# The running streams' stage of a hybrid encoder step: its tiles, its head loads, and the place of the filler and of the first two rows

## The chip, the cores and the metric

The kernel runs on one core of one Trainium2 chip. The metric is the device time of one execution in microseconds. The kernel before was timed three times, and its median is what a changed kernel is set against. One further execution was profiled.

The engines have short names: PE multiplies matrices (PEld is its weight load), DVE, ACT and POOL work on vectors, and SP issues nearly all DMA transfers. Each engine takes its instructions strictly in its program's order and waits at an instruction until its inputs and its buffer are there.

## The reference, cut to what matters

One step of a one-layer encoder for two groups of requests that share the weights: a prompt of 1,040 rows (16 meta rows and 1,024 frames), and 8 running streams with 16 new frames each, which have 272 cached rows of keys and values (16 meta, 256 past). Attention is stick-breaking, with 16 heads of 64:

```python
def stick_breaking(q, k, v, q_pos, k_pos):
    z = jnp.einsum('bqhd,bshd->bhqs', q, k) * (SB_HEAD_DIM ** -0.5)
    reach = k_pos[None, :] < q_pos[:, None]
    log_beta = jax.nn.log_sigmoid(z)
    log_keep = jnp.where(reach, jax.nn.log_sigmoid(-z), 0.0)
    later = lax.cumsum(log_keep, axis=3, reverse=True) - log_keep
    w = jnp.where(reach, jnp.exp(log_beta + later), 0.0)
    return jnp.einsum('bhqs,bshd->bqhd', w, v)
```

Beside it runs a Mamba-2 scan (SSD) over the same rows. Its output is gated, normed and projected by `w_br_ssd`; attention's by `w_br_att`; two sigmoid gates weigh the sum, `w_out` projects it, and a causal convolution FFN follows. For a stream, attention goes over 272 cached and 16 new keys.

## The kernel before, in words

Every float32 product is made of three: a number x is split into a rounded part h (a cast on ACT) and the rest l (a subtraction on DVE), and `mm3` multiplies h by h, h by l and l by h. `weights` loads a block of 128 columns (`wf`) and splits it into `wh` and `wl`.

The phases follow each other: norm and the first projections (`norm_in`), the SSD, the prompt's attention (`phase_att`), the streams' attention (`phase_smp`), the merge (`ssd_operands` builds the operands of `w_br_ssd`, `br_ssd` multiplies), the FFN. A scheduler lays out the instructions of each engine; tiles come from pools that are stacked, so a tile of a later phase lies over tiles of an earlier one and its first write waits for their last use. Which tiles those are is set by the order in which the pools are made.

**The prompt's attention** goes head by head. `head` (L690) loads KH and KL (the split keys), QS (the split queries) and makes VV (the split values), each from a pool of two buffers. It works on 8 blocks of 128 rows, four to a group. For a block i PE makes z (L719, L722), ACT takes the sigmoid into `beta` (L682), POOL masks its diagonal (L728) and makes `keep` = 1 - beta (L685), DVE runs the product scan (L686) and multiplies (L688). Then, for a group, PV: for each j PE transposes the betas (L135, wT), ACT and DVE split them (L97, L98), PE multiplies (L743, L744), and a short tail goes through `wf` (L749, L751).

**Filler.** `self.fill` is a list of projection blocks that attention does not need: keys, queries and values of later head pairs, and 16 blocks of the gate logits (`gate`). A gate block is 72 matmuls, three tiles of 24, and each tile's result goes through ACT (L670) into `s_gate`. `paced` (L966) takes blocks from the list after each head and ties a tile to a mark, one of the z matmuls, behind which it may start. The rest of the list goes to the streams' stage; the last `RESERVE` = 3 blocks are kept for its end.

**The streams' stage.** `first_queries` (L758) handles the first two rows of the prompt, which see at most 15 keys: it loads 16 keys and 2 queries of all heads, makes z, a small stick-breaking in `fb`, and 8 products with `fw` (L796). `sample_att` (L802) then loads the queries (`qhs`, `qls`), the new keys of all streams (`kxh`, `kxl`, 16 loads, L813), and the last 16 cached keys of each stream (`last`, 2 times 8 loads, L819), which PE transposes and ACT and DVE split into kx in pieces of 128 columns. For each stream and half it loads 256 rows of the cache (`ck` tiles from a pool of four buffers), transposes and splits the keys into Ksh and Ksl, to which POOL copies the 32 last keys from kx (L860), spreads the queries into a block-diagonal `qd`, and runs z, the stick-breaking and PV. The results are gathered in `od` and `aout`, and `aout` is stored in one transfer (L916). `norm_rows` (L924) turns the SSD's row sums `s_ss` into factors `r`, by a square root on ACT, for which ACT loads a table, and three Newton steps on DVE, and writes `s_rs`.

**The merge's operands.** For each of 16 blocks `ssd_operands` loads yt (L939, two buffers), multiplies by rB (L941), and scales into sh on ACT (L942) and sl on DVE (L943).

## Time and profile before

| what | value |
|---|---|
| median of 3 runs | 3040.69 us (3036.63 to 3044.58) |
| profiled execution | 3035.7 us, span 3033.7 us |
| mean granted clock of PE in it | 0.988 |
| last z matmul of head 15 | 1478.93 us |
| first filler of the streams' stage | 1517.00 us |
| last matmul of the streams' stage ends, reserved filler begins | 1694.57 us |
| `w_br_ssd` begins | 1732.82 us |

A row of the timeline reads: start, duration, engine, line, operation, output <- inputs, shapes, number of merged instructions, and in brackets how long the engine had been idle before it and who ended that. A line number in a row is one of the kernel before. Durations of matmuls overlap, so their spacing says more than their length: the filler's matmuls of 384 columns last 0.34 us each and start 0.178 us apart at full clock.

### The profile page before, as it was taken

To read this page: it belongs to the slowest core of one execution; us is meant where nothing else is said; L and a number is where in the kernel's file an instruction comes from. 1 tells how busy PE (TensorE), PEld (TensorE's weight loads), DVE (VectorE), ACT (ScalarE), POOL (GpSimd) and SP (SyncE) were. 2 spreads that over 40 slices of the span, in tenths; PEclk is the share of its full clock that TensorE was granted. 3 is DMA by queue.
4 is the path that set the end of the run, shared out by engine and by line. 5 is a ranking of instruction groups with operands and counts; after the bars stand their busy time and mean duration, and the time that the engine had idled before them with its cause. 6 is when DMAs were issued, how large, how long until landed. Compare 5 with 4: busy or idle time off the path is not lost. (4 is left out here: it accounts for less than half of the span.)

```text
span 3033.7 us, 45461 instructions
## 1 busy us (share of the span) xinstructions
PE 2926.8 (96%) x17381; PEld 2768.3 (91%) x17381; DVE 1733.1 (57%) x2625; ACT 1262.9 (42%) x2630; POOL 611.2 (20%) x967
## 2 busy tenths in 40 slices
PE   7999999999989999999799899999999999999998
PEld 5997988979879999999699899999999999999997
DVE  6467666666656777777634441346754454545447
ACT  6545435354334544554434320214534242424245
POOL 0013132131222333333323000002201010101014
PEclk9999999999999999999899999999999999999999
DMA  5436255353574554544444553536211111111113
GB/s 188 110 86 172 87 141 152 91 162 90 148 218 125 167 148 132 157 124 106 77 137 140 168 171 100 152 105 195 71 43 44 43 44 43 44 43 40 39 43 119
DMA packets 445496, 338.44 MB, mean 112 GB/s; under 512 B 43991, under 2 KB 421155, under 8 KB 445279
## 3 DMA queue, kind: packets, MB, share of 16 engines
q1 hardware_dynamic: 445279, 335.54, 38.8%
q8 instruction: 137, 2.24, 0.3%
q14 instruction: 80, 0.66, 0.1%
HBM read 244.31 MB, written 91.15 MB: 111 GB/s over the span
## 5 line engine op out<-in xcount | busy, mean ns | idle before, releaser
L115 PE MATMUL mm<-sh,wh 128*128 128x384 f32 (+3 forms) x2520 | 869.5, 346 | 14.7 <-ACT sh L942 5.2
L118 PE MATMUL mm<-sl,wh 128*128 128x384 f32 (+3 forms) x2520 | 869.8, 345 | 2.3 <-DVE sl L98 1.2
L119 PE MATMUL mm<-sh,wl 128*128 128x384 f32 (+3 forms) x2520 | 865.6, 344 | 0.0
L115 PEld LDWEIGHTS mm<-sh,wh 128*128 128x128 f32 (+1 forms) x2520 | 475.7, 189 | 29.5 <-ACT sh L942 6.4
L118 PEld LDWEIGHTS mm<-sl,wh 128*128 128x128 f32 (+1 forms) x2520 | 475.7, 189 | 15.5 <-issue 8.9
L119 PEld LDWEIGHTS mm<-sh,wl 128*128 128x128 f32 (+1 forms) x2520 | 475.5, 189 | 5.7 <-issue 3.9
L106 DVE TENSOR_TENSOR wl<-wf,wh 128x1024 fp32r<-128x1024 f32 (+2 forms) x205 | 252.6, 1233 | 318.0 <-ACT wh L105 317.8
L115 PE MATMUL mm<-ph,wh 128*128 128x386 f32 x1248 | 424.5, 340 | 2.7 <-ACT ph L97 2.0
L118 PE MATMUL mm<-pl,wh 128*128 128x386 f32 x1248 | 424.6, 341 | 0.0
L119 PE MATMUL mm<-ph,wl 128*128 128x386 f32 x1248 | 422.5, 339 | 0.2 <-DVE wl L106 0.2
L105 ACT CAST wh<-wf 128x1024 fp32r<-128x1024 f32 (+2 forms) x205 | 212.4, 1037 | 482.2 <-PE mm L118 454.5
L1151 DVE SCALAR_TENSOR_TENSOR acc<-fx,cwf,acc 128x256 f32<-128x256 f32 (+1 forms) x352 | 170.8, 516 | 154.0 <-ACT acc L1149 150.0
L115 PEld LDWEIGHTS mm<-ph,wh 128*128 128x128 f32 x1248 | 236.2, 189 | 3.9 <-ACT ph L97 2.3
L119 PEld LDWEIGHTS mm<-ph,wl 128*128 128x128 f32 x1248 | 236.2, 189 | 1.1 <-DVE wl L106 0.7
L118 PEld LDWEIGHTS mm<-pl,wh 128*128 128x128 f32 x1248 | 235.2, 188 | 1.8
L686 DVE TENSOR_TENSOR_SCAN keep<-keep 128x144 f32<-128x144 f32 (+7 forms) x128 | 179.7, 1406 | 57.9 <-POOL keep L685 57.2
L115 PE MATMUL mm<-ah,wh 128*128 128x384 f32 x528 | 179.8, 340 | 0.0
L119 PE MATMUL mm<-ah,wl 128*128 128x384 f32 x528 | 179.2, 339 | 0.0
L118 PE MATMUL mm<-al,wh 128*128 128x384 f32 x528 | 178.6, 338 | 0.0
L1078 POOL TENSOR_TENSOR sq<-sq,sq 128x386 f32<-128x386 f32 (+1 forms) x42 | 60.2, 1434 | 467.9 <-ACT sq L1077 456.4
L98 DVE TENSOR_TENSOR wTl<-wT,wTh 128x512 fp32r<-128x512 f32 (+3 forms) x176 | 103.0, 602 | 80.1 <-ACT wTh L97 79.1
L1176 DVE TENSOR_TENSOR h<-mm,h 128x384 f32<-128x384 f32 x144 | 79.8, 556 | 119.7 <-PE mm L119 119.5
(329 smaller groups left out, 4548.2 us busy)
## 6 DMA issues: line engine op xcount, KB each, us to landing
wf<-in_w_in SPq DMA_DIRECT2D x80, 512.0 KB
wf<-in_w_up SPq DMA_DIRECT2D x44, 512.0 KB
t<-s_ac SPq DMA_DIRECT2D x36, 512.0 KB
wf<-in_w_down SPq DMA_DIRECT2D x28, 512.0 KB
wf<-in_w_out SPq DMA_DIRECT2D x24, 512.0 KB
s_y<-x SPq DMA_DIRECT2D x16, 577.0 KB
yt<-s_y SPq DMA_DIRECT2D x16, 577.0 KB
KH<-s_kh SPq DMA_DIRECT2D x32, 260.0 KB
```

Source lines behind the costliest of these rows:

```text
L98: nc.vector.tensor_tensor(out=l, in0=x, in1=h.bitcast(F32), op=ALU.subtract)
L105: nc.scalar.copy(wh, wf)
L106: nc.vector.tensor_tensor(out=wl, in0=wf, in1=wh.bitcast(F32), op=ALU.subtract)
L115: i = nc.tensor.matmul(p, wh[:, k, :], mh[:, c:c + w], start=s, stop=False)
L118: nc.tensor.matmul(p, wh[:, k, :], ml[:, c:c + w], start=False, stop=False)
L119: nc.tensor.matmul(p, wl[:, k, :], mh[:, c:c + w], start=False, stop=e)
L686: nc.vector.tensor_tensor_scan(out=K[:, ::-1], data0=K[:, ::-1], data1=K[:, ::-1], initial=1.0, op0=ALU.mult, op1=ALU.min)
L1078: nc.gpsimd.tensor_tensor(out=acc[:, :w], in0=acc[:, :w], in1=sq, op=ALU.add)
L1151: nc.vector.scalar_tensor_tensor(out=op, in0=src(q), scalar=w(q), in1=op, op0=ALU.mult, op1=ALU.add)
L1176: self.nc.vector.tensor_tensor(out=h, in0=p, in1=h, op=ALU.add)
```

## The change

1. A scratch tile `s_ck` in DRAM gets the rows 256 to 272 of all streams' cached keys, by one copy of 512 KB whose place in the code is behind head 1. `last` is then loaded from it, 2 loads for 16.
2. kx becomes two pairs: kc for the cached keys, kn for the new ones. kn comes by 2 loads of all streams for 16 loads; kc is split 512 columns at a time; POOL copies two pieces of 16 keys for one of 32.
3. KH, KL, QS and VV get a pool for even and one for odd heads, one buffer each. The pools of both stages are made in another order: the streams' first tiles (`last`, qd, qs, kn, kc) lie over tiles of the last but one head, and `mixst`, `od` and `aout` come last.
4. `first_queries` is called ahead of head 15 and takes three of the four `ck` buffers for its tiles.
5. `RESERVE` is 2, and one gate block runs at the end of head 15: its first tile may start behind the last mark (z of row block 6), the second and third behind the first PV matmul of group 0 and of group 1 (`pv_marks`).
6. `norm_rows` is called ahead of `sample_att`.
7. The pool `rows` is made ahead of the pool `fill`.

```diff
-RESERVE = 3
+RESERVE = 2
...
+        self.s_ck = dr([TS, 1024], 's_ck')
...
-        KH, KL = (self.tile(ap, [128, TP], F32R, n) for n in ('KH', 'KL'))
-        QS = self.tile(ap, [128, TP - T0], F32R, 'QS')
-        VV = self.tile(ap, [128, 9, 128], F32R, 'VV')
+        KH, KL = (self.tile(ap, [128, TP], F32R, f'{n}{h % 2}', bufs=1) for n in ('KH', 'KL'))
+        QS = self.tile(ap, [128, TP - T0], F32R, f'QS{h % 2}', bufs=1)
+        VV = self.tile(ap, [128, 9, 128], F32R, f'VV{h % 2}', bufs=1)
...
-                nc.tensor.matmul(po[:, lo:], VV[:, j, :], wh[:, lo:], start=(j == 0), stop=False)
+                mm = nc.tensor.matmul(po[:, lo:], VV[:, j, :], wh[:, lo:], start=(j == 0), stop=False)
+                if j == 0:
+                    self.pv_marks = [mm] if g == 0 else self.pv_marks + [mm]
...
-        x = self.tile(ap, [128, 4, 288], F32R, 'Ksh').bitcast(F32).rearrange("p a b -> p (a b)")[:, :288]
+        x, v, Q = (self.tile(self.ckp, [128, 2, 512], F32, 'ck').rearrange("p a b -> p (a b)") for _ in range(3))
...
-        for j in range(8):
-            for t, src in zip(kx, (self.s_kh, self.s_kl)):
-                nc.sync.dma_start(t[:, j, :, 16:32].bitcast(F32),
-                                  src[128 * j:128 * j + 128, TP:T].rearrange("p (b t) -> p b t", t=16))
+        kc, kn = ([self.tile(ap, [128, 8, TS], F32R, n + x, bufs=1) for x in 'hl'] for n in ('kc', 'kn'))
+        for t, src in zip(kn, (self.s_kh, self.s_kl)):
+            nc.sync.dma_start(t.bitcast(F32), src[:, TP:T].rearrange("(j p) t -> p j t", p=128))
...
-            for b in range(NB):
-                nc.sync.dma_start(lk[16 * b:16 * b + 16], ck[b, 256:272, 512 * hf:512 * hf + 512])
+            nc.sync.dma_start(lk, self.s_ck[:, 512 * hf:512 * hf + 512])
...
-            for j in range(4):
-                self.split(h[:, j], l[:, j], v[:, j])
+            self.split(*(t[:, 4 * hf:4 * hf + 4] for t in kc), pk.rearrange("p (j s) -> p j s", j=4))
...
-                    nc.gpsimd.tensor_copy(K[:, :, 256:288], kx[x][:, 4 * hf:4 * hf + 4, b].bitcast(F32))
+                    for i, k in enumerate((kc, kn)):
+                        nc.gpsimd.tensor_copy(K[:, :, 256 + 16 * i:272 + 16 * i],
+                                              k[x][:, 4 * hf:4 * hf + 4, 16 * b:16 * b + 16].bitcast(F32))
...
-                'wTh', 'wTl', 'wf32', 'att', 'vf', 'KH', 'KL', 'QS', 'VV', 'keep', *(f'beta{i}' for i in range(8)))}
+                'KH0', 'KL0', 'QS0', 'VV0', 'vf', *(f'beta{i}' for i in range(8)), 'KH1', 'KL1', 'QS1', 'VV1', 'keep',
+                'wTh', 'wTl', 'wf32', 'att', 'fb', 'fw', 'fo')}
...
+                    if p == 7 and e == 1:
+                        self.first_queries()
...
-        self.ckp = self.pool(right, "cache", 4, side='right')
+                        self.ckp = self.pool(right, "cache", 4, side='right')
+                        self.nc.sync.dma_start(self.s_ck.rearrange("(b s) c -> b s c", s=16),
+                                               self.a['cache_k'][0, :, 256:272].rearrange("b s h d -> b s (h d)"))
+            self.fill.pop(0)([marks[-1]] + self.pv_marks)
...
-            mp = self.stp = self.pool(c2, "mixst", 3)
...
-                'aout', 'od', 'wTh', 'wTl', 'keep', 'beta', 'v', 'r', 'newton', 'qdh0', 'qhs', 'qls', 'kxh', 'kxl',
-                'last', 'V3h', 'V3l', 'qdl0', 'qdh1', 'qdl1', 'Ksh', 'Ksl', 'Vsh', 'Vsl',
-                'w30', 'w31', 'fb', 'fw', 'fo')}
+                'last', 'qdh0', 'qdl0', 'qdh1', 'qdl1', 'qhs', 'qls', 'knh', 'knl', 'kch', 'kcl', 'Ksh', 'Ksl', 'V3h', 'V3l',
+                'v', 'r', 'newton', 'beta', 'keep', 'Vsh', 'Vsl', 'w30', 'w31', 'wTh', 'wTl', 'od', 'aout')}
+            self.stp = self.pool(c2, "mixst", 3)
...
-            self.first_queries()
+            self.norm_rows(self.ap)
             self.sample_att(3 * len(self.fill) / 16)
-            self.norm_rows(self.ap)
...
+                k.rowp = k.pool(c1, "rows", 2)
                 k.stp = k.pool(c1, "fill", 7)
-                k.rowp = k.pool(c1, "rows", 2)
```

**PE at the end of head 15.** The numbers behind a name tell its buffers apart. Before, behind the last two z matmuls (L719, L722) stand group 0's last PV matmuls, the transposes of both groups and nothing else:

```order
L719 MATMUL z_15646<-KH_15486,QS_15488 128x344
L722 MATMUL z_15646<-KL_15487,QS_15488 128x344
L744 MATMUL o_15549<-wTl_15567,VV_15489 128x400
L135 MATMUL wT_15582<-ident_60,beta_2879_15523 128x128
L135 MATMUL wT_15582<-ident_60,beta_2882_15534 128x128 x2
L743 MATMUL o_15549<-wTh_15576,VV_15489 128x272
L135 MATMUL wT_15659<-ident_60,beta_2899_15594 128x128
L135 MATMUL wT_15659<-ident_60,beta_2903_15609 128x128
L135 MATMUL wT_15659<-ident_60,beta_2907_15624 128x128
L744 MATMUL o_15549<-wTl_15577,VV_15489 128x272
L751 MATMUL o_15549<-wf_2897_15586,VV_15489 128x144
L751 MATMUL o_15549<-wf_2897_15586,VV_15489 128x16
```

In the changed kernel the same z matmuls (now L720, L723) are followed by matmuls of a gate block (`mm`, L115 to L119), among which the PV and the transposes stand:

```order
L720 MATMUL z_15716<-KH_2879_15556,QS_2881_15558 128x344
L723 MATMUL z_15716<-KL_2880_15557,QS_2881_15558 128x344
L115 MATMUL mm_15913<-sh_124,wh_15908 128x384
L118 MATMUL mm_15913<-sl_125,wh_15908 128x384
L119 MATMUL mm_15913<-sh_124,wl_15909 128x384
L115 MATMUL mm_15913<-sh_126,wh_15908 128x384
L747 MATMUL o_15619<-wTl_15626,VV_2882_15559 128x512
L135 MATMUL wT_15642<-ident_60,beta_2886_15582 128x128
L135 MATMUL wT_15642<-ident_60,beta_2889_15593 128x128
L135 MATMUL wT_15642<-ident_60,beta_2892_15604 128x128
L118 MATMUL mm_15913<-sl_127,wh_15908 128x384
```

So filler now stands between the last z and the transposes that need the last beta.

**PE at the head of the streams' stage.** Before, from the last tail product of head 15 (L751) to the first filler:

```order
L751 MATMUL o_15658<-wf_2939_15739,VV_15489 128x144
L751 MATMUL o_15658<-wf_2939_15739,VV_15489 128x16
L779 MATMUL z_15966<-Ksh_15954,last_15962 32x16 x8
L135 MATMUL pk_16030<-ident_60,last_16021 128x128 x4
L135 MATMUL wT_15981<-ident_60,fb_15975 16x32
L796 MATMUL o_15985<-fw_15983,Vsh_15959 128x32 x8
L135 MATMUL pk_16052<-ident_60,last_16043 128x128 x4
L135 MATMUL pk_16115<-ident_60,ck_16103 128x128 x4
L879 MATMUL z_16134<-Ksh_16107,qdh_2968_16065 128x288
L115 MATMUL mm_16188<-sh_119,wh_16183 128x384
```

Now, from the same product (L754):

```order
L754 MATMUL o_15728<-wf_2949_15809,VV_2882_15559 128x144
L754 MATMUL o_15728<-wf_2949_15809,VV_2882_15559 128x16
L135 MATMUL pk_16141<-ident_60,last_16139 128x128 x4
L135 MATMUL pk_16150<-ident_60,last_16148 128x128 x4
L135 MATMUL pk_16209<-ident_60,ck_16195 128x128 x4
L135 MATMUL pk_16216<-ident_60,ck_16195 128x128 x4
L877 MATMUL z_16228<-Ksh_16199,qdh_2984_16157 128x288
L115 MATMUL mm_16282<-sh_120,wh_16277 128x384
```

The first two rows' z, transposition and eight products are gone from here, and both halves of `last` are transposed at once.

**ACT at the same place.** Before, `norm_rows`' table load and square root (L925) stand behind all of head 15:

```order
L749 COPY wf_2939_15739<-wT_15735 128x272
L872 CAST Vsh_16129<-ck_16105 128x1024
L753 COPY att_15743<-o_15658 64x512
L925 ACT_TABLE_LOAD
L925 ACTIVATE r_17935<-v_17934,eps_69 64x73
L783 ACT_TABLE_LOAD
L783 ACTIVATE fb_15975<-z_15966 32x16
L97 CAST kxh_16003<-pk_16030 128x8x16 x3
```

Now they (L923) stand between the last beta's sigmoid (L683) and group 0's tail `wf` (L752):

```order
L683 ACTIVATE beta_2921_15709<-z_15713 128x348
L683 ACTIVATE beta_2921_15709<-z_15716 128x344
L97 CAST wTh_15646<-wT_15642 128x272
L923 ACT_TABLE_LOAD
L923 ACTIVATE r_16116<-v_16115,eps_69 64x73
L671 ACT_TABLE_LOAD
L671 ACTIVATE st_15938<-mm_15913 128x384
L752 COPY wf_2907_15656<-wT_15652 128x272
L756 COPY att_15660<-o_15619 64x512
L97 CAST wTh_15734<-wT_15729 128x512
```

Behind them on ACT stand a gate tile's evacuation (`st`) and both groups' remaining copies.

**SP at the end of the streams' stage.** Before, the store of `aout` (L916) stands ahead of the first rB and yt:

```order
L104 DMA wf_18381<-in_w_br_ssd 128x8x128
L104 DMA wf_20719<-in_w_out 128x8x128
L104 DMA wf_20754<-in_w_out 128x8x128
L916 DMA s_att_86<-aout_15998 128x8x128
L936 DMA rB_18261<-s_rs_85 128x1154
L939 DMA yt_18263<-s_y_83 128x1154
L939 DMA yt_18270<-s_y_83 128x1154
L671 DMA s_gate_87<-st_18022 128x384
```

Now rB and the first two yt (L934, L937) stand ahead of the weights of `w_out` and of the store (L914):

```order
L104 DMA wf_18482<-in_w_br_ssd 128x8x128
L934 DMA rB_18281<-s_rs_86 128x1154
L937 DMA yt_18283<-s_y_84 128x1154
L937 DMA yt_18290<-s_y_84 128x1154
L104 DMA wf_20739<-in_w_out 128x8x128
L104 DMA wf_20774<-in_w_out 128x8x128
L914 DMA s_att_87<-aout_16128 128x8x128
L937 DMA yt_18297<-s_y_84 128x1154
```

The second pair of yt stays behind the store.

More of the change, by code (lines that the diff above doesn't have):

```diff
@@ L760, in first_queries @@
         nc, ap, pa = self.nc, self.ap, self.pa
-        x = self.tile(ap, [128, 4, 288], F32R, 'Ksh').bitcast(F32).rearrange("p a b -> p (a b)")[:, :288]
-        x = x.rearrange("p (i j t) -> p i j t", i=2, j=8)
+        x, v, Q = (self.tile(self.ckp, [128, 2, 512], F32, 'ck').rearrange("p a b -> p (a b)") for _ in range(3))
+        x = x[:, :288].rearrange("p (i j t) -> p i j t", i=2, j=8)
         for i, (qs, ks) in enumerate(((self.s_qh, self.s_kh), (self.s_ql, self.s_kl))):
@@ L765, in first_queries @@
             nc.sync.dma_start(x[:, i, :, 2:18], ks[:, 0:16].rearrange("(j p) t -> p j t", p=128))
-        v = self.tile(ap, [128, 2, 512], F32R, 'Vsh').bitcast(F32)[:16].rearrange("p a (j c) -> p (a j) c", c=128)
+        v = v[:16].rearrange("p (j c) -> p j c", c=128)
         nc.sync.dma_start(v, self.s_v[:, 0:16].rearrange("j t c -> t j c"))
         nc.vector.tensor_tensor(out=x[:, 0], in0=x[:, 0], in1=x[:, 1], op=ALU.add)
-        Q = self.tile(ap, [128, 512], F32, 'last', bufs=2)[:, :256].rearrange("p (j c) -> p j c", c=32)
+        Q = Q[:, :256].rearrange("p (j c) -> p j c", c=32)
         nc.gpsimd.memset(Q, 0.0)
@@ L776, in first_queries @@
             nc.gpsimd.tensor_copy(diagonal(Q.rearrange("p j c -> p (j c)"), e), x[64 * e:64 * e + 64, 0, :, 0:2])
-        ps = self.tile(pa, [128, 512], F32, 'z')
+        ps = self.tile(pa, [128, 512], F32, 'z', bufs=2)
         for j in range(8):
@@ L793, in first_queries @@
         nc.scalar.copy(w, pt[:16, :32])
-        po = self.tile(pa, [128, 512], F32, 'o')
+        po = self.tile(pa, [128, 512], F32, 'o', bufs=2)
         for j in range(8):
@@ L808, in sample_att @@
             nc.sync.dma_start(t.bitcast(F32), src[:, TP - T0:T2].rearrange("(j p) t -> p j t", p=128))
-        kx = [self.tile(ap, [128, 8, NB, 32], F32R, n, bufs=1) for n in ('kxh', 'kxl')]
-        for j in range(8):
-            for t, src in zip(kx, (self.s_kh, self.s_kl)):
-                nc.sync.dma_start(t[:, j, :, 16:32].bitcast(F32),
-                                  src[128 * j:128 * j + 128, TP:T].rearrange("p (b t) -> p b t", t=16))
+        kc, kn = ([self.tile(ap, [128, 8, TS], F32R, n + x, bufs=1) for x in 'hl'] for n in ('kc', 'kn'))
+        for t, src in zip(kn, (self.s_kh, self.s_kl)):
+            nc.sync.dma_start(t.bitcast(F32), src[:, TP:T].rearrange("(j p) t -> p j t", p=128))
         for hf in range(2):
             lk = self.tile(ap, [128, 512], F32, 'last', bufs=2)
-            ck = a['cache_k'][0].rearrange("b s h d -> b s (h d)")
-            for b in range(NB):
-                nc.sync.dma_start(lk[16 * b:16 * b + 16], ck[b, 256:272, 512 * hf:512 * hf + 512])
+            nc.sync.dma_start(lk, self.s_ck[:, 512 * hf:512 * hf + 512])
             pk = self.tile(pa, [128, 512], F32, 'pk', bufs=2)
```

2 lines of the change are left out of this document (removed).

## The prediction

> **What bounds the kernel now.** I read the profile's page first, then the busy time by windows, the timeline of TensorE (PE) where the windows show holes, and the lists of the other engines for who ended each wait. The page:
>
> ```profile
> PE 2926.8 (96%) x17381; PEld 2768.3 (91%) x17381; DVE 1733.1 (57%) x2625; ACT 1262.9 (42%) x2630; POOL 611.2 (20%) x967
> PEclk9999999999999999999899999999999999999999
> ```
>
> PE is busy 96% of the span and no other engine comes near. The change takes no PE work away, so it can only win where PE idles or runs at a lower granted clock. The only slice of the clock line below 9 lies in the middle, where the last head of the prompt hands over to the running streams' stage. There the windows read (busy time of each engine, granted clock, DMA share, GB/s):
>
> ```profile
> core 0: us, PE busy (x) PEld busy (x) DVE busy (x) ACT busy (x) POOL busy (x), PEclk, DMA share, GB/s
> 1480.00:1490.00 10.00, 5.18 (x25) 3.49 (x25) 7.73 (x8) 2.04 (x4) 3.87 (x5) 0.85 1.01 138
> 1490.00:1500.00 10.00, 7.87 (x33) 6.06 (x33) 3.22 (x6) 3.42 (x7) 0.41 (x2) 0.64 0.76 78
> 1500.00:1510.00 10.00, 1.66 (x25) 1.28 (x23) 3.70 (x12) 4.73 (x9) 3.88 (x8) 0.70 0.64 168
> 1510.00:1520.00 10.00, 8.97 (x36) 8.46 (x36) 3.17 (x8) 3.74 (x11) 3.17 (x7) 0.50 0.25 41
> ```
>
> Busy time times clock is 4.4 + 5.0 + 1.2 + 4.5 = 15.1 us of full-speed work in 40 us: 24.9 us are lost. With a few tenths on either side this hole costs about 26 us (the clock is not weighted by busy time, so 24 to 28). PE's timeline through it:
>
> ```profile
> 1477.79 0.40 PE L743 MATMUL o<-wTh,VV 128*128 128x512 f32 x1
> 1478.93 0.32 PE L722 MATMUL z<-KL,QS 128*128 128x344 f32 x1
> ...
> 1486.61 0.45 PE L135 MATMUL wT<-ident,beta 128*128 128x128 f32 x2 [3.13 <-DVE beta L688]
> 1487.62 0.80 PE L743 MATMUL o<-wTh,VV 128*128 128x512 f32 x1 [0.56 <-ACT wTh L97]
> ...
> 1493.86 0.79 PE L744 MATMUL o<-wTl,VV 128*128 128x512 f32 x1 [1.74 <-DVE wTl L98]
> ...
> 1501.90 0.63 PE L135 MATMUL pk<-ident,last 128*128 128x128 f32 x4 [0.99 <-DMA last<-in_cache_k]
> 1509.87 0.21 PE L135 MATMUL wT<-ident,fb 32*16 32x32 f32 x1 [7.34 <-DVE fb L789]
> 1510.34 3.62 PE L796 MATMUL o<-fw,Vsh 16*128 16x32 f32 x16 [0.26 <-ACT fw L793]
> ...
> 1516.62 0.58 PE L879 MATMUL z<-Ksh,qdh 128*128 128x288 f32 x1 [0.77 <-ACT Ksh L97]
> 1517.00 0.52 PE L115 MATMUL mm<-sh,wh 128*128 128x384 f32 x1
> ...
> 1521.11 0.34 PE L118 MATMUL mm<-sl,wh 128*128 128x384 f32 x1
> ...
> 1522.00 0.34 PE L115 MATMUL mm<-sh,wh 128*128 128x384 f32 x1
> ```
>
> Head 15 has no filler. After its last z matmul (1478.93) PE waits for the last row block's chain on POOL and DVE until 1486.61. Then come its seven PV steps without cover, and the first two rows' little attention, which holds PE 7.34 us for `fb`. Filler begins at 1517.00, at half clock. From 1521.11 to 1522.00 five filler matmuls start, 0.178 us each, so a gate block of 72 is 12.8 us of cover.
>
> **Term 1, the last head and the stage's head.** The change puts one gate block into the hole. Its first tile comes behind row block 6's z and spreads over the 7.4 us up to 1486.61: some 32 filler matmuls (5.7 us) and group 0's own PV work fill that. The rest stands between the last transposes and the first two PV steps. The first two rows' matmuls (2.5 us or so of work) go ahead of head 15, into filler of head 14 and 15, and the 7.34 us wait for `fb` goes with them. ACT and DVE carry less there too:
>
> ```profile
> 1499.50 1.05 ACT L872 CAST Vsh<-ck 128x1024 fp32r<-128x1024 f32 x1
> ...
> 1505.33 1.28 ACT L925 ACT_TABLE_LOAD   x1 [4.17 <-DMA v<-s_ss]
> ...
> 1515.89 0.59 ACT L97 CAST Ksh<-pk 128x512 fp32r<-128x512 f32 x1 [0.19 <-PE pk L135]
> ```
>
> ```profile
> 1495.38 4.93 SPq L819 DMA_DIRECT2D last<-in_cache_k  x8
> ...
> 1501.50 0.47 SPq L924 DMA_DIRECT2D v<-s_ss  x1
> ```
>
> Two loads from the scratch tile replace the two rows of eight (4.93 us of issue for one of them), two loads of 512-byte runs replace sixteen of 64-byte runs, and the splits of kx go from four a half to one.
>
> What stays lost afterwards, worked out: (i) five full PV steps of group 1 nearly without filler, each a hand-over PE to ACT (0.59) to DVE to PE, with a weight split (1.05 on ACT) among them: 3 us, bounds 1.5 and 6, from the single wait of 1.74 above taken once to three times. (ii) The hand-over to the first stream: behind the last PV matmul ACT copies `att`, casts two Vsh (2 x 1.05) and two kch (2 x 0.59), then Ksh (0.59), about 4.4 us in order, with only transposes for PE: 4 us, bounds 2 and 6. (iii) Filler at half clock behind it: before, the 13 starts from 1517.00 to 1521.11 took 4.1 us instead of 2.3, so 1.8 us (0 to 3.6). That is 9 us, so the term is 26 - 9 = **-17 us**, bounds -24 (28 less 4) and -11.
>
> Whether (iii) is due hangs on how long a gap must be. Before, the gap of 3.13 us was followed by a 512-column matmul of 0.80 us where the same took 0.40 at 1477.79. The Trainium skill ("TensorE: Matmul & The Clock Gate", What's actually happening) says that the clock falls to half after an idle window of about 3.4 us, the window running free. By that rule a gap that I have at 4 us may or may not hold a whole window, and the sum would be 1.8 us lower where it doesn't; the trace's gap of 3.13 us, with shorter ones around it, was enough, so I keep the cost.
>
> **Term 2, norm_rows in the last head.** Its chain cost ACT 1.28 + a second table load + the wait for `v`: issued at 1501.50, ACT free at 1505.33, 3.8 us. Now ACT sits there behind the last z, ahead of group 0's `wf`, and DVE's r steps stand ahead of all wTl of group 1. From the last z to the first PV of group 1 PE has some 39 filler matmuls (6.9 us) and about 2.6 us of group 0's work and transposes, 9.5 us; ACT's way is 3.8 + 1.28 + 0.4 + 1.28 and three copies of about 0.5, 8.3 us. Hidden with about 1 us to spare: 0, bounds 0 and +4.
>
> **Term 3, the merge head.** Two blocks instead of three are left to cover the building of w_br_ssd's operands. Before:
>
> ```profile
> 1735.00:1740.00 5.00, 2.33 (x10) 1.31 (x8) 3.06 (x3) 1.64 (x2) 0.00 (x0) 0.95 0.81 285
> 1740.00:1745.00 5.00, 2.65 (x9) 2.57 (x9) 3.64 (x3) 2.58 (x3) 0.00 (x0) 0.50 0.85 254
> 1745.00:1750.00 5.00, 5.00 (x27) 5.00 (x26) 1.36 (x1) 1.13 (x1) 0.00 (x0) 0.87 1.02 345
> ```
>
> ```profile
> 1680.13 0.29 PE L883 MATMUL z<-Ksh,qdl 128*128 128x288 f32 x1
> ...
> 1694.57 0.42 PE L115 MATMUL mm<-sh,wh 128*128 128x384 f32 x1
> ...
> 1769.76 0.44 PE L115 MATMUL mm<-sh,wh 128*128 128x384 f32 x1 [1.22 <-ACT sh L942]
> ```
>
> ```profile
> 1695.31 0.37 SPq L916 DMA_DIRECT2D s_att<-aout  x1
> ...
> 1701.52 0.81 SPq L939 DMA_DIRECT2D yt<-s_y  x2
> 1702.38 7.02 SPq L671 DMA_DIRECT2D s_gate<-st  x2
> ```
>
> ```profile
> 1709.29 1.26 ACT L942 ACTIVATE sh<-yt,gv 128x1154 fp32r<-128x1154 f32 x1 [0.24 <-DVE yt L941]
> ```
>
> ```profile
> 1709.18 2.84 DVE L943 SCALAR_TENSOR_TENSOR sl<-yt,gv,sh 128x1154 fp32r<-128x1154 f32 x2
> ```
>
> The same product gives 2.2 + 1.3 + 4.4 = 7.9 us of work in 15: 7.1 lost, plus 1.22: 8.3 us. One block less takes away 12.8 us of cover. What pays for it: `aout`, `od` and `mixst` move to the end of the stage's stack, so the first two yt loads no longer stand behind the store of `aout` (1695.31, which before they followed by 6.2 us) but wait for the last z (1680.13). Two yt buffers make a chain of pairs. Before, the first pair was done at 1709.18 + 2.84 = 1712.0, 17.4 us behind the stage's end at 1694.57. Now yt times rB can be done before the end, and what is left behind the last copies of `aout` (about 0.5) is one sh of 1.26, beside the second of which the two sl of 1.42 begin, 4.6 us in all: 12.8 us earlier. Later pairs gain more if SP is not held at the gate stores as at 1702.38 (7.02 us): up to 19 us earlier. Lost afterwards 8.3 + 12.8 - (12.8 to 19) = 8.3 to 2.1, middle 5: **-3 us**, bounds -8.3 (nothing lost) and +12.8 (no load earlier).
>
> **Term 4, the start.** The copy into `s_ck` (512 KB) waits for nothing, and its issue stands ahead of the loads of x, on which PE waits:
>
> ```profile
> 14.70 2.10 SPq L238 DMA_DIRECT2D x<-in_x_prompt  x3
> ```
>
> ```profile
> 20.39 0.55 PE L135 MATMUL tp<-ident,x 128*128 128x128 f32 x3 [1.71 <-DMA x<-in_x_prompt]
> ```
>
> ```profile
> 10.00:20.00 10.00, 8.03 (x35) 5.73 (x33) 7.58 (x30) 8.70 (x22) 0.39 (x2) 1.00 0.86 243
> ```
>
> At 243 GB/s 512 KB are 2.2 us of a transfer that is 0.86 busy already: **+2 us**, bounds 0 (other matmuls fill it) and +4 (read and write both counted). The Trainium skill ("DMA: Bandwidth & Descriptors", Rules for kernel authors) speaks against this form: an outermost dimension of fewer than 16 confines a transfer to that many engines, and this one has 8. By it the copy takes twice as long but leaves eight engines free; the sum would stay inside those bounds, and no row here shows such a copy.
>
> **Edits at nothing.** 32 more POOL copies, each half as wide as this one:
>
> ```profile
> 1520.45 0.29 POOL L860 CAST Ksh<-kxh 128x128 fp32r<-128x128 f32 x1 [3.19 <-ACT kxh L97]
> ```
>
> At most 32 x 0.29 = 9.3 us over the stage's 174 us (1521 to 1694.57), on an engine at 20% overall; without cover they would cost PE at most that. I take 0, -2 to +2. The heads' two pools by parity hold the same two buffers. The new order of att's pools shifts head 0's loads at the SSD's end, where PE loses time already:
>
> ```profile
> 840.00:850.00 10.00, 4.90 (x31) 2.57 (x32) 5.10 (x11) 8.92 (x23) 1.18 (x2) 0.83 0.49 135
> ```
>
> That 5.10 us of missing PE time can shrink or grow by most of itself: 0, -4 to +4.
>
> **The sum.** -17 + 0 - 3 + 2 + 0 = -18. The profiled run took 3035.7 us (span 3033.7 and 2.0 around it), 5.0 below the median of the three shown, 3040.7. So 3035.7 - 18 = 3017.7 on its own scale, and **3022.7 us**, say 3023, against the median. A difference of 0.3%, 9.1 us, is about what can be told from none: faster means under 3031.6, slower over 3049.8.
>
> **The rivals.**
> (a) *The cover is missed at the merge.* The yt loads come no earlier, because what they now lie over is released late, or the queue is held at a weight load ahead of them: +12.8 instead of -3, so -18 + 15.8 = -2, 3038. For it: SP issues in order and was held 7.02 us at 1702.38. Against: in the new order the first yt loads stand ahead of the w_out weights and the `aout` store. Chance 0.1.
> (b) *The hole stays.* The new tiles still wait for head 15, or the PV tail and hand-over are at the long ends of (i) and (ii), so half of 17 is won: -9.5, 3031, on the edge of no change. For it: `knl` and `qhs` are still loaded behind the last z. Against: `last` and its two splits no longer wait for anything of head 15. Chance 0.12.
> (c) *The slow side: ACT held at the load of `v` in the last head.* ACT runs in order; while it waits for `v`, it evacuates neither `wf` nor filler nor wTh, and PE starves once the 1 us to spare is used. `v` is issued behind a cache load, the store of `fo` and a weight load. Every us past 3.8 + 1 = 4.8 costs one; slower than before by 9.1 needs 18 + 9.1 = 27 of them, a wait of 32 us. At 40 us: 35 - 18 = +17, 3058. For it: all loads of this place share one queue, and a weight load ahead of `v` has to find its buffer free. Against: the wait of before was 4.17 (row at 1505.33). Chance 0.06, with anything else on that side.
> (d) *It does not do what it says*: PE's order keeps the filler out of the hole. Against: the order of PE's program has those matmuls there. Chance 0.02, 3040 or above.
>
> **How the numbers follow.** The forecast's own case has 0.70. Half the widths of its terms are 6.5, 2, 5.5, 2, 2 and 4 us; they are independent, so the root of the sum of squares, 10 us, is what they make together: 3013 to 3033. To leave out no more than 2 in 10 of all cases the range goes half as far again: 3008 to 3037, which takes in nearly all of the own case (0.67), most of (b) and the near part of (a). Faster: 0.64 of the 0.70 lies under 3031.6, half of (b) and a third of (a) with a larger term 1: 0.73. Same: the rest of these three and (d), 0.06 + 0.06 + 0.07 + 0.02 = 0.21. Slower: (c), 0.06.
>
> **What would show it.** Right: from the last z of head 15 to full-clock filler in the streams' stage PE is busy at clock 1.00 but for about 9 us, with no wait for `fb`; one gap of about 4 us ahead of the first z of stream 0; yt's first loads issued before the store of `aout`; waits in w_br_ssd of about 5 us. Wrong: a wait of ACT for `v` above 5 us with PE idle behind it; the first yt load behind the stage's end; a transposition of x waiting more than 4 us at the start; or gaps grown elsewhere inside the streams' stage.

## The result, and the profile after

The changed kernel takes 3003.75 us (median of 5 runs, 3002.16 to 3011.89), the kernel before 3040.56 us (5 runs, 3036.45 to 3044.58). The ratio is 0.9885, with a 95% interval from 0.9867 to 0.9903: about 37 us faster, twice what was forecast and 4 us below the range's lower end (two more comparisons of the same program, e12 and e3 below, give 32 and 31 us). The profiled execution took 3004.2 us; its span, 3002.4, is 31.3 shorter than that of before. The page of the changed kernel:

```profile
PE 2915.3 (97%) x17381; PEld 2763.2 (92%) x17381; DVE 1729.5 (58%) x2619; ACT 1262.0 (42%) x2624; POOL 614.6 (20%) x999
PEclk9999999999999999999999999999999999999998
```

PE does the same matmuls, and the slice below 9 in the middle is gone. Where the time went is read by following the same matmul through both profiles. Each row of the table is the start of one matmul; the offset is after minus before, and the last column is how much the offset changed since the row above.

| matmul | before | after | offset | change of this part |
|---|---|---|---|---|
| first transposition of the SSD (`sio`) | 126.1 | 128.4 | +2.3 | +2.3 |
| its last transposition of `cs` | 755.7 | 757.0 | +1.3 | -1.0 |
| first PV of attention (wTh, VV) | 929.5 | 924.0 | -5.5 | -6.8 |
| last z of head 15 | 1478.9 | 1476.6 | -2.3 | +3.2, holds the first two rows' matmuls, 2.5 or so |
| first z of the streams | 1516.6 | 1507.3 | -9.3 | -7.0, holds one block more (12.8) |
| last transposition of the stage | 1694.2 | 1681.1 | -13.1 | -3.8 |
| first norm sum of the FFN | 2089.1 | 2057.4 | -31.7 | -18.6, holds one block less |

So, with the block's 12.8 us put to one side: start +2.3, the SSD and its end -7.8, the last head and the stage's head -16.6, the stage -3.8, the merge -5.8: -31.7.

PE through the former hole, in the changed kernel (the rows that answer to those of before from the last z on):

```profile
1476.60 0.32 PE L723 MATMUL z<-KL,QS 128*128 128x344 f32 x1
...
1486.22 0.64 PE L754 MATMUL o<-wf,VV 128*128 128x144 f32 x4 [1.32 <-ACT wf L752]
...
1500.14 1.07 PE L135 MATMUL pk<-ident,last 128*128 128x128 f32 x8
1504.19 1.25 PE L135 MATMUL pk<-ident,ck 128*128 128x128 f32 x8 [2.98 <-DVE kcl L98]
1507.27 0.61 PE L877 MATMUL z<-Ksh,qdh 128*128 128x288 f32 x1 [1.82 <-POOL Ksh L857]
...
1512.47 0.37 PE L115 MATMUL mm<-sh,wh 128*128 128x384 f32 x1
1512.68 0.34 PE L118 MATMUL mm<-sl,wh 128*128 128x384 f32 x1
```

No wait for the last beta and none for `fb` is left. Three waits above 0.3 us are: one for ACT's `wf`, and two in the hand-over to the first stream, 4.8 us together, behind which filler runs at half clock (granted clock 0.50) until 1512.47. The windows (columns as before):

```profile
1475.00:1485.00 10.00, 9.91 (x62) 9.34 (x61) 7.61 (x10) 4.45 (x9) 1.35 (x2) 1.00 0.57 125
1485.00:1495.00 10.00, 8.74 (x54) 8.13 (x54) 3.40 (x9) 4.68 (x10) 0.00 (x0) 1.00 0.18 54
1495.00:1505.00 10.00, 6.71 (x41) 5.02 (x42) 6.55 (x10) 6.55 (x12) 5.88 (x17) 1.00 0.56 153
1505.00:1515.00 10.00, 8.18 (x37) 7.94 (x36) 2.67 (x4) 2.30 (x4) 3.16 (x9) 0.66 0.53 164
```

By busy time times clock 0.1 + 1.3 + 3.3 + 4.6 = 9.3 us are lost in 40 (9.2 in finer windows, where the kernel before loses 25.8 from 1475 to 1525 us by the same count; 7.7 in e12).

ACT behind the last z, with `norm_rows` in it, and the first yt loads at the stage's end on SP, whose last z starts at 1666.5:

```profile
1478.63 1.28 ACT L923 ACT_TABLE_LOAD   x1
1483.73 0.36 ACT L923 ACTIVATE r<-v,eps 64x73 f32<-64x73 f32 x1 [3.82 <-DMA v<-s_ss]
1484.11 1.28 ACT L671 ACT_TABLE_LOAD   x1
1485.40 0.49 ACT L671 ACTIVATE st<-mm 128x384 f32<-128x384 f32 x1
1485.79 0.38 ACT L752 COPY wf<-wT 128x272 f32<-128x272 f32 x1
```

```profile
1663.33 0.32 SPq L934 DMA_DIRECT2D rB<-s_rs  x1
1666.66 0.80 SPq L937 DMA_DIRECT2D yt<-s_y  x2
1667.51 4.09 SPq L104 DMA_DIRECT2D wf<-in_w_out  x2
1682.21 0.37 SPq L914 DMA_DIRECT2D s_att<-aout  x1
```

The two yt loads are issued right behind the last z and 15.6 us ahead of the store. In the merge PE then waits four times for under 0.9 us instead of 1.65, 1.02, 2.35 and 1.22. Then the start, and the window in the SSD's end, for which the prediction had taken no change:

```profile
25.01 0.90 PE L135 MATMUL tp<-ident,x 128*128 128x128 f32 x3 [4.29 <-DMA x<-in_x_prompt]
```

```profile
840.00:850.00 10.00, 7.99 (x59) 5.93 (x58) 5.46 (x11) 7.71 (x22) 3.43 (x4) 1.00 0.70 194
```

The matmul behind that hole, first before, then after:

```profile
845.41 2.05 PE L473 MATMUL st<-xe,bt 128*128 128x512 f32 x2 [5.10 <-ACT bt L456]
```

```profile
844.81 1.10 PE L474 MATMUL st<-xe,bt 128*128 128x512 f32 x2 [2.02 <-issue]
```

PE waits 4.29 us for x at the start where it waited 1.71, and the hole at 845 us is 2.0 instead of 5.1 us. Before, half clock follows it (matmuls of 2.05 us together where they now take 1.10), so the window loses 2.0 us of work now and lost 5.9.

### The profile page after: what moved, and what is told of

Its sections match the earlier page's. It is cut to its first block, busy times and chain, and to the rows that moved or that the text cites. A ratio compares the mean times of both kernels' runs of the same rounds, so it can differ in the third digit from the quotient of the medians.

```text
span 3002.4 us, 45455 instructions
## 1 busy us (share of the span) xinstructions
PE 2915.3 (97%) x17381; PEld 2763.2 (92%) x17381; DVE 1729.5 (58%) x2619; ACT 1262.0 (42%) x2624; POOL 614.6 (20%) x999
## 4 chain that ended last, share of the span: by engine, by line
PE 80%; DMA 8%; DVE 5%; ACT 3%; issue 2%; POOL 1%; SPq 0%; POOLq 0%; ACTq 0%; DVEq 0%
PE mm L115 22%; PE mm L118 22%; PE mm L119 22%; PE wT L135 3%; DMA t<-s_ac 2%; DMA yt<-s_y 1%; PE yd L489 1%; PE z L720 1%; PE o L747 1%; PE z L723 1%; DMA out_ssm_sample<-t 1%; PE o L744 1%; PE st L474 1%; DMA wf<-in_w_out 1%; PE px L135 1%
## 5 line engine op out<-in xcount | busy, mean ns | idle before, releaser
L115 PE MATMUL mm<-sh,wh 128*128 128x384 f32 (+3 forms) x2520 | 866.7, 345 | 9.2 <-ACT xp L369 3.7
L119 PE MATMUL mm<-sh,wl 128*128 128x384 f32 (+3 forms) x2520 | 865.2, 344 | 0.0
L115 PEld LDWEIGHTS mm<-sh,wh 128*128 128x128 f32 (+1 forms) x2520 | 474.6, 188 | 22.3 <-issue 5.9
L119 PEld LDWEIGHTS mm<-sh,wl 128*128 128x128 f32 (+1 forms) x2520 | 475.0, 188 | 5.6 <-issue 3.9
L115 PE MATMUL mm<-ph,wh 128*128 128x386 f32 x1248 | 424.4, 340 | 2.0 <-ACT ph L97 2.0
L119 PE MATMUL mm<-ph,wl 128*128 128x386 f32 x1248 | 422.6, 339 | 1.1 <-DVE wl L106 1.1
L1155 DVE SCALAR_TENSOR_TENSOR acc<-fx,cwf,acc 128x384 f32<-128x384 f32 (+2 forms) x352 | 170.8, 515 | 154.6 <-ACT acc L1153 150.6
L115 PEld LDWEIGHTS mm<-ph,wh 128*128 128x128 f32 x1248 | 236.2, 189 | 2.9 <-ACT ph L97 2.3
L119 PEld LDWEIGHTS mm<-ph,wl 128*128 128x128 f32 x1248 | 236.2, 189 | 1.8 <-DVE wl L106 1.4
L115 PE MATMUL mm<-ah,wh 128*128 128x384 f32 x528 | 179.8, 340 | 0.0
L119 PE MATMUL mm<-ah,wl 128*128 128x384 f32 x528 | 179.2, 339 | 0.0
```

The lines of the kernel that those rows point to most:

```text
L115: i = nc.tensor.matmul(p, wh[:, k, :], mh[:, c:c + w], start=s, stop=False)
L119: nc.tensor.matmul(p, wl[:, k, :], mh[:, c:c + w], start=False, stop=e)
L1155: nc.vector.scalar_tensor_tensor(out=op, in0=src(q), scalar=w(q), in1=op, op0=ALU.mult, op1=ALU.add)
```

## The experiments

All ratios are to the kernel before, timed anew on the same chip in each comparison; between the comparisons its median moves from 3033.1 to 3040.6 us. Offsets are those of the profiled run to the kernel before, as in the table.

**The block (e1).**

```diff
-RESERVE = 2
+RESERVE = 3
...
-            self.fill.pop(0)([marks[-1]] + self.pv_marks)
```

> The changed kernel without the gate block at the end of head 15, and with three blocks reserved again. Theory A (the block is what fills the hole): the time lost by PE between the last z of head 15 and full-clock filler, 9 us in the changed kernel, grows by 10 to 13 us, the merge head loses its 3 us less, and the time is 7 to 10 us above the changed kernel's. Rival B (the early loads, the merged splits and the moved queries made the gain, and the block only stands in for waits that are gone anyway): the head loses at most 4 us more, and the time is within 2 us of the changed kernel's.

Ratio 0.9924 (0.9909 to 0.9939), 3012.0 us. The profiled run took 3012.0, 8 us above the changed kernel's. PE waits again where it did:

```profile
1480.33 0.64 PE L754 MATMUL o<-wf,VV 128*128 128x144 f32 x4 [2.68 <-ACT wf L752]
1485.98 0.69 PE L135 MATMUL wT<-ident,beta 128*128 128x128 f32 x2 [4.41 <-DVE beta L689]
...
1501.24 1.79 PE L135 MATMUL pk<-ident,ck 128*128 128x128 f32 x8 [3.70 <-DVE kcl L98]
```

Windows from 1475 to 1525 us lose 17.1 us instead of 9.2 (7.7 in e12): theory A for the hole, with 8 to 9 us for the growth, a little less than its 10. The other half of the hole's 16.6 us was won without the block. And the merge, with its third block back, waits no less (1.75 and 1.28 us): so a third block there would win nothing.

**The first two rows (e2).**

```diff
-                    if p == 7 and e == 1:
-                        self.first_queries()
...
+            self.first_queries()
             self.norm_rows(self.ap)
```

> The changed kernel with the first two rows' attention called at the head of the streams' stage again. Theory A (its chain of waits is not covered there): 5 to 10 us above the changed kernel, with a wait for fb of several us on PE behind the last PV. Rival B (the hand-over to the first stream, about 5 us of PE waiting anyway, hides the chain): at most 2 us above it, no more than its 2.5 us of matmuls.

Ratio 0.9923 (0.9908 to 0.9938), 3012.1 us. From the first PV of attention to the stage's end it takes 3.7 us longer than the changed kernel's first profile, and 6.9 longer than that of e12. Both programs have the rows' matmuls in this stretch, so the difference lies in waits and in half clock:

```profile
1505.51 0.18 PE L135 MATMUL wT<-ident,fb 32*16 32x32 f32 x1 [1.18 <-POOL Ksl L857]
1508.72 0.58 PE L877 MATMUL z<-Ksh,qdh 128*128 128x288 f32 x1 [3.02 <-ACT Ksh L97]
```

There is no 7-us wait for `fb`: with its loads long done, the chain mostly lies beside the hand-over, as B had it. The total would speak for A, but nearly 4 us of it stand ahead of the first PV, where both programs are the same, and 3 in the merge. So the move itself is worth 4 to 7 us at its place, in one profile against two.

**norm_rows (e3).**

```diff
-            self.norm_rows(self.ap)
             self.sample_att(3 * len(self.fill) / 16)
+            self.norm_rows(self.ap)
```

> The changed kernel with norm_rows called behind the streams' attention again, as before. Theory A (its wait for v and its steps are hidden in the last head): within 2 us of the changed kernel, and PE's gap ahead of the tail product of group 0 (1.3 us) goes. Rival B (its place costs the last head, as the slow side of the prediction had it): 2 to 5 us below the changed kernel. Rival C (its table loads and wait then fall into the hand-over to the first stream): 3 to 6 us above.

Ratio 0.9904 (0.9884 to 0.9923), 3006.0 us; the profiled span is 1.8 us longer. But the edit changes nothing: the scheduler laid out the same list of instructions on every engine, and `norm_rows`' square root on ACT still stands in head 15, at 1482.9. So none of the theories is tested, and the run is one more profile of the changed kernel. PE's wait for `wf` is only 0.17 us there because `v` came earlier (ACT waits 2.68 us for it instead of 3.82); the two of the hand-over are 2.98 and 2.31. Item 6 of the change thus has no effect by itself beside the other items.

**The pools of attention, alone (e4).** The kernel before with these lines of the change:

```diff
+        KH, KL = (self.tile(ap, [128, TP], F32R, f'{n}{h % 2}', bufs=1) for n in ('KH', 'KL'))
+        QS = self.tile(ap, [128, TP - T0], F32R, f'QS{h % 2}', bufs=1)
+        VV = self.tile(ap, [128, 9, 128], F32R, f'VV{h % 2}', bufs=1)
...
+                'KH0', 'KL0', 'QS0', 'VV0', 'vf', *(f'beta{i}' for i in range(8)), 'KH1', 'KL1', 'QS1', 'VV1', 'keep',
+                'wTh', 'wTl', 'wf32', 'att')}
...
+                k.rowp = k.pool(c1, "rows", 2)
                 k.stp = k.pool(c1, "fill", 7)
```

> The kernel before with only the tiles' overlay at the start of attention changed: KH, KL, QS and VV in pools by parity of the head, the order of attention's pools, and rows ahead of fill. Theory A (these pools alone let head 0's loads start earlier at the SSD's end): PE's loss between 840 and 950 us falls from 14 to about 9 us, the time is 6 to 8 us below the kernel before, all of it by the first PV matmul. Rival B (the gain there comes from the scheduler's other order, set off by the scratch copy or the moved queries): within 2 us of the kernel before.

Ratio 1.0022 (1.0012 to 1.0031): slower. But at the first PV of attention the offset is -6.5 us, and the window of the hole reads:

```profile
840.00:850.00 10.00, 8.11 (x57) 5.77 (x56) 5.60 (x9) 8.74 (x23) 3.46 (x3) 1.00 0.64 193
```

So theory A holds at its place, and its total is wrong: with the streams' pools in their old order the gain is lost again at the end of attention. They now lie over other tiles there, which is the likely reason but was not tested alone. The last z of head 15 stands at -2.3, the first z of the streams at +4.1, behind a longer wait for the last beta (3.13 us before) and a new one for `last`:

```profile
1488.50 0.69 PE L135 MATMUL wT<-ident,beta 128*128 128x128 f32 x2 [6.91 <-DVE beta L688]
...
1506.62 1.04 PE L779 MATMUL z<-Ksh,last 128*32 128x16 f32 x16 [7.47 <-POOL last L776]
```

What shrank the hole can be seen on ACT. Its list there is held at the load of `t` (9.07 us before, 8.06 in the changed kernel); PE's matmul of `bt` comes behind it. Before:

```profile
840.41 2.44 ACT L483 ACTIVATE t<-t,tok 128x128 f32<-128x128 f32 x8 [9.07 <-DMA t<-s_ac]
842.76 1.03 ACT L105 CAST wh<-wf 128x1024 fp32r<-128x1024 f32 x1
843.69 0.48 ACT L560 ACTIVATE st<-mm 128x386 f32<-128x386 f32 x1
844.08 1.04 ACT L484 ACTIVATE t<-t 128x1024 f32<-128x1024 f32 x1
845.02 0.24 ACT L456 COPY bt<-ms 128x128 f32<-128x128 f32 x1
```

After:

```profile
832.07 1.05 ACT L105 CAST wh<-wf 128x1024 fp32r<-128x1024 f32 x1
833.01 0.50 ACT L561 ACTIVATE st<-mm 128x386 f32<-128x386 f32 x1
...
842.12 2.44 ACT L484 ACTIVATE t<-t,tok 128x128 f32<-128x128 f32 x8 [8.06 <-DMA t<-s_ac]
844.47 0.24 ACT L457 COPY bt<-ms 128x128 f32<-128x128 f32 x1
844.61 1.05 ACT L485 ACTIVATE t<-t 128x1024 f32<-128x1024 f32 x1
```

The scheduler laid the engines' lists out anew, and `bt` came to stand right behind the step that waits: of the three longer steps that stood between, two now go ahead of the wait and one behind `bt`. ACT has the same order in e4. That the lists changed because attention's first tiles became free at other times is how the scheduler works out its times, and not shown by a run of its own.

**The copy into s_ck (e5).**

```diff
+                        self.issue_after(cp, marks[-1])
```

> The changed kernel with the copy into s_ck tied behind the last z mark of head 1, so that its issue stands in the middle of attention and not at the start. Theory A (the copy's bytes, ahead of the loads of x, cost 2 to 4 us at the start): 2 to 3 us below the changed kernel, with the offset gone by 130 us. Rival B (the start lost time by a chance reordering or by the load of the memory): within 1 us of it.

Ratio 0.9893 (0.9877 to 0.991), 3004.3 us. At its place theory A holds: PE waits 1.79 us for x instead of 4.29, and the offset at 126 us is -1.1 instead of +2.3. In the total nothing of these 3.4 us is seen. They are gone by the first PV of attention (offset -4.8, the changed kernel's -5.5), where the same matmuls come at other times from profile to profile; and the merge is 4.5 us longer than in the first profile of the changed kernel, whose repetition (e12) is 2.7 longer there too. The cause at the start stands firm even so: in the eleven profiles with the copy there, e12 among them, the offset at 126 us is +0.6 to +4.0, and in the three without it (before, e4, e5) -1.1 to +0.8.

**rB and the yt loads (e6).**

```diff
+            if g == 0:
+                self.issue_after(d, self.att_store)
...
+                if b < 2:
+                    self.issue_after(d, self.att_store)
```

> The changed kernel with the first rB and the first two yt loads ordered behind the store of aout on SP again, all else as it is. Theory A (these loads' place pays for the block that is missing at the merge): the merge head is 8 to 13 us longer, and so the time. Rival B (the operands' chain is held elsewhere, by its later pairs or by ACT's order with the gate evacuations): at most 4 us longer.

Ratio 0.992 (0.9898 to 0.9941), 3011.8 us. rB and the first two yt stand behind the store, these at 1683.5:

```profile
1683.49 1.11 SPq L939 DMA_DIRECT2D yt<-s_y  x2
1686.76 8.30 SPq L672 DMA_DIRECT2D s_gate<-st  x2
```

The offset is -12.9 at the stage's end, as in the changed kernel, and -23.0 at the FFN's first norm sum where that has -31.7. The merge is 8.5 us longer: theory A. The order in which three loads are issued is worth that much.

**rows and fill (e8).**

```diff
-                k.rowp = k.pool(c1, "rows", 2)
                 k.stp = k.pool(c1, "fill", 7)
+                k.rowp = k.pool(c1, "rows", 2)
```

> The changed kernel with the pool rows behind the pool fill, as before, so that the streams' first tiles (last, qs) lie over other tiles, and last is loaded behind the last head's filler. Theory A (the early loads of last matter): the wait ahead of the first transposes at the streams' head grows, 2 to 5 us above the changed kernel. Rival B (last is there in time all the same): within 1.5 us. For the gain at the SSD's end, 5 us of PE's loss between 840 and 950: if it stays, it belongs to the pools of KH, KL, QS and VV; if it goes, to the place of rows.

Ratio 0.9906 (0.9884 to 0.9927), 3005.4 us, the profiled span 0.1 us from the changed kernel's. `last` is waited for (1.89 us), but the wait behind it is 1.47 instead of 2.98, and the other is gone: B. From 755 us to the first PV of attention it wins 5.4 us, so that gain does not need `rows` in its new place: with e4 it belongs to attention's own pools. Whether to the pairs by parity or to the order of the others was not separated.

**The third tile later (e9), and qhs early (e11, e10).** e9 lets the third tile start behind group 1's last product:

```diff
-                if j == 0:
-                    self.pv_marks = [mm] if g == 0 else self.pv_marks + [mm]
+                if j == 0 and g == 0:
+                    self.pv_marks = [mm]
...
+            if g == 1:
+                self.pv_marks = self.pv_marks + [mm]
```

e11 only reorders the streams' pools; e10 does both.

```diff
-                'last', 'qdh0', 'qdl0', 'qdh1', 'qdl1', 'qhs', 'qls', 'knh', 'knl', 'kch', 'kcl', 'Ksh', 'Ksl', 'V3h', 'V3l',
-                'v', 'r', 'newton', 'beta', 'keep', 'Vsh', 'Vsl', 'w30', 'w31', 'wTh', 'wTl', 'od', 'aout')}
+                'last', 'V3h', 'V3l', 'w30', 'w31', 'beta', 'keep', 'qhs', 'qls', 'v', 'r', 'newton', 'qdh0', 'qdl0', 'qdh1', 'qdl1',
+                'knh', 'knl', 'kch', 'kcl', 'Ksh', 'Ksl', 'Vsh', 'Vsl', 'wTh', 'wTl', 'od', 'aout')}
```

> The changed kernel with the third tile of the last head's gate block allowed only behind the last product of group 1, so that its 24 matmuls (4.3 us) stand in the hand-over to the first stream. Theory A (what is left of the hole is that hand-over, two waits of 3.0 and 1.8 us and the half clock behind them, and PV hardly needs the tile): 2 to 5 us below the changed kernel. Rival B (PV of group 1 then waits as long): within 1.5 us. Rival C (ACT's evacuation of that tile lengthens the hand-over): above it.

> The changed kernel with another order of the streams' pools: V3h, V3l, w30, w31, beta and keep, which are needed late, take the place over the filler's tiles, and qhs, qls and the tiles of norm_rows the place behind it, so that qhs is loaded ahead of the last head's end. Theory A (the second wait of the hand-over, 1.8 us for POOL's copies into Ksh, stands behind POOL's work on the queries and goes): 1 to 3 us below the changed kernel. Rival B (the hand-over is set by ACT's order of copies alone): within 1 us.

> As the last, and with the third tile of the block behind the last product of group 1. Theory A (where that tile was late before, the gain was eaten by the wait of 3.2 us for qd, whose load of qhs stood behind the tile's store on SP; loaded early, the tile covers the hand-over): 3 to 6 us below the changed kernel. Rival B (ACT, which evacuates the tile and splits in the same order, stays late): within 1.5 us.

Ratios 0.9905 (0.9886 to 0.9925), 0.9918 (0.9903 to 0.9933) and 0.9926 (0.9909 to 0.9944): none is better than the changed kernel, and e11 and e10 are worse, by 6 and 8 us against e12 on the same chip, which fits none of their theories. e9 lies 2 to 3 us above, as C had it, but not for ACT: the tile moves the wait on to POOL, whose load of qhs stands behind the tile's store on SP:

```profile
1512.14 0.61 PE L879 MATMUL z<-Ksh,qdh 128*128 128x288 f32 x1 [3.18 <-POOL qdh L863]
```

```profile
1503.07 0.38 SPq L672 DMA_DIRECT2D s_gate<-st  x1
1507.42 0.38 SPq L813 DMA_DIRECT2D qhs<-s_qh  x1
```

In e10 the hand-over itself is nearly covered (waits of 1.95 and 0.17 us, 4.5 us lost from 1475 to 1525 instead of 9.2). But `norm_rows`, with its table loads on ACT, comes to stand in the midst of head 15, which loses 3.5 us before 1475 (3.7 in e11), and at the stage's end the first block of w_out is loaded late, ACT stands at its cast, and PE at ACT:

```profile
1678.93 1.04 ACT L105 CAST wh<-wf 128x1024 fp32r<-128x1024 f32 x1 [6.21 <-DMA wf<-in_w_out]
1679.89 0.58 ACT L906 COPY od<-o 128x512 f32<-128x512 f32 x1
```

```profile
1680.52 1.12 PE L135 MATMUL wT<-ident,od 128*128 128x128 f32 x4 [5.21 <-ACT od L906]
```

**A third order (e13).** The later tile of e9, and this order:

```diff
+                'last', 'kch', 'kcl', 'keep', 'w30', 'w31', 'qhs', 'qls', 'qdh0', 'qdl0', 'qdh1', 'qdl1',
+                'knh', 'knl', 'Ksh', 'Ksl', 'V3h', 'V3l', 'v', 'r', 'newton', 'beta', 'Vsh', 'Vsl', 'wTh', 'wTl', 'od', 'aout')}
```

> The changed kernel with the third tile of the block behind the last product of group 1, and the streams' pools in a third order: kch, kcl, keep, w30 and w31 over the filler's tiles, qhs and qls behind them, the tiles of norm_rows late, so that its load of v comes no earlier than in the changed kernel. Theory A (the two kernels with early qhs won 2 to 4 us in the hand-over and lost it where norm_rows' wait moved ahead into head 15, and where the weights of w_out came late and held ACT, and so PE, for 5 us at the stage's end; without these two the gain stays): 2 to 5 us below the changed kernel. Rival B (another overlay only moves the waits again): within 2 us or above.

Ratio 0.9921 (0.9905 to 0.9938): B. The two losses of e10 are gone (2.55 us is the longest wait at the stage's end). ACT now waits 5.44 us for `v` in head 15, and PE 2.90 for `wf` behind it (3.82 and 1.32 in the changed kernel), but kch now lies over the filler's tiles, whose store it must wait for:

```profile
1511.56 1.07 ACT L97 CAST kch<-pk 128x512 fp32r<-128x512 f32 x2 [5.68 <-DMA s_gate<-st]
```

PE waits 7.60 us for the split behind it.

**The changed kernel again (e12).** No edit.

> The changed kernel once more, for its scatter beside the kernel before on one chip, and for the scale on which a profiled run stands to a median. Theory A (of the 37 us between the two medians about 5 belong to the run of before that was profiled, which lay below its median): the ratio is between 0.988 and 0.991, 27 to 36 us, and the profiled run lies within 3 us of the first one's 3004.4 with the same losses by stage. Rival B: the ratio is 0.9885 or less again, and the profiled runs understate the gain.

Ratio 0.9897 (0.9883 to 0.9912), 3004.9 against 3036.9 us, 32 us: theory A for the times. The profiled span is 3004.3. Its stages are not the same each: it shows +0.6 at the start, -5.3 at the SSD's end, the heads within 1.5 us of the first profile, and the stage and merge together within 1 us of the first profile, though not each alone: merge -3.2 where the first has -5.8.

## Why the prediction was wrong

The direction was right, and so were the mechanisms of the terms that were worked from rows, and their totals; the items of term 1 were not. The number was 19 us too high; the range missed by 4.

- *Term 1, -17 us:* -16.6. What was to stay lost, 9 us, is 9.2, but that the sum fits so closely is luck, as its items miss both ways: the PV steps lose 0.2 (forecast 3), the hand-over's two waits 4.8 (forecast 4), half clock behind them 2.6 (forecast 1.8), and 1.3 go to the wait for `wf`, which term 2 had at nothing. Half clock came though no gap was long by itself: 2.98, then 1.25 us of transposes, then 1.82. That the block makes this gain was half true: e1 gives it 8 us, and 8.7 are won without it. Moving the first two rows is worth 4 to 7 us over the whole stretch (e2); that the loads and the splits made the rest is argued, as no run takes them alone.
- *Term 2, 0:* ACT waited 3.82 us for `v` (forecast 3.8), hidden but for 1.3 us, where 1 us to spare had been forecast. How much is hidden can be read, as the wait varies from run to run: at 2.68 us (e3), 2.79 (e12), 3.41 (e6), 3.82 and 5.44 (e13) PE waits 0.17, 0.28, 0.91, 1.32 and 2.90 us for `wf`. So 2.5 us are hidden and every further one costs one. The place of the call in the code has no part in it, as e3 has the same lists.
- *Term 3, -3 us:* -5.8 in the first profile, -3.2 in e12, -5.6 in e3. That the place of the yt loads pays for the missing block is shown by e6 (8.5 us). The working set cover against the operands' chain, and that is the balance; in e1 a third block buys nothing there.
- *Term 4, +2 us:* +2.3 (+0.6 in e12, +1.7 in e3), and e5 ties it to the copy. The wait for x of 4.29 us that I had named as a sign against me did come, and other matmuls filled part of it.
- *The step that failed* is the one on attention's pools under "Edits at nothing": "0, -4 to +4" for the SSD's end. It is -6.8, and -5.3 in e12; in the eleven profiles with this program up to there it lies between -3.3 and -7.2, -5.4 in the middle. I priced only the loads of head 0 and took the middle. The overlay also changed the order of ACT's list in the SSD's last group, so that `bt` comes sooner behind the step that waits: the hole shrank from 5.10 to 2.02 us (2.29 in e12). e4 and e8 tie this to attention's pools. Up to 1.7 us of the -6.8 are luck: no half clock follows the hole in the first profile, and in seven of the eleven, e12 among them, it does. The 5.10-us hole with its half clock stood in the window that I quoted, so the term could have been bounded at -6, but its sign not known from the diff.
- *Inside the stage* 0 was forecast and -3.8 came (-5.6 in e12, -1.9 in e3; at the stage's end e12 has no stretch at half clock, the first profile one of 3.4 us and e3 two). PE loses 2.8 us instead of 5.9 from 1525 to 1660 us. Why stays open, as no run separates it: fewer waits for Ksh and for cache loads are what the lists show.
- *The scale.* I added 5.0 us because the profiled run lay below the median of three. The medians of before in the later comparisons are 3035.0, 3037.2, 3036.9 and 3033.1: the profiled run's 3035.7 was in their midst, and the first median, 3040.7, lies above all of them. So the first median seems to have been the one off; why it lay higher is open. Without the 5 us the forecast would have been 3017.7 and the range would have held 3003.75 only just (3003 to 3032).
- *The range* was narrower than its own terms allow. Term 3 went into the root with 5.5 us, but half the distance of its bounds (-8.3 and +12.8) is 10.5; with that the root is 13.4 us instead of 10, and the range 3003 to 3043. Term 1's upper bound, -11, also does not follow from its items: at their long ends they add up to 15.6 us, which leaves -8 to -10.

So 5.0 of the 19 us are the scale, and the rest is 7.8 from the SSD, 3.8 from the stage and 2.8 from the merge.

Of the rivals, (c) was right in kind and wrong in place. Its price of one us for one is what the waits under term 2 show, but beyond 2.5 us and not beyond 4.8; the wait stayed short, so it cost 1.3 us. e10 and e13 show what a wait of ACT for a transfer does elsewhere when an order goes wrong, 5 to 8 us each.

## What to carry to other kernels

A pool's place in the stack decides when the next stage's first tile may be written, and where a scheduler lays out the engines' lists, it changes them in the stage ahead too: after a change of overlay look at every place where PE idled before, with a bound as large as that idling, and not only at the tiles that moved. An overlay is right only as a whole: a part of this one was slower than none (e4), and of four variants that were to shorten single waits in it (e9, e10, e11, e13) none was faster: they moved the waits. Look at the engines' lists before a variant is timed: one whose lists are the same (e3) tests nothing. Price a hole by what stands in it and what will stand behind it, and compare item by item afterwards: here the total held to half a microsecond while one item was 3 us and another 1 us off.
